# The first tile's load of a rotary-embedding kernel, issued as two partition halves on two DMA queues

## The chip, the core and the metric

The kernel runs on one core of one Trainium2 chip. The metric is the device time of one execution in microseconds (us). Repeated executions (five of the kernel before) took 162.28 to 162.43 us. Kernels are compared only within the same rounds. The span of the profiled execution is about 2 us shorter than the time (160.4 us against 162.38).

## The reference

Each of 16 x 512 positions holds 16 heads of 64 numbers (float32). The first 32 numbers of a head are rotated with a cosine and a sine of the position; the last 32 pass through.

```python
batch, seq, heads, dim = (16, 512, 16, 64)          # x: 33.5 MB
x1, x2 = x[..., :32], x[..., 32:]
rotated_first  = x1[..., :16] * cos[..., :16] - x1[..., 16:] * sin[..., :16]
rotated_second = x1[..., :16] * sin[..., :16] + x1[..., 16:] * cos[..., :16]
return concatenate([rotated_first, rotated_second, x2], axis=-1)
```

## The kernel before

x is cut into 8 tiles of 4 MiB. A tile in SBUF, the core's on-chip memory, takes 128 partitions, with one contiguous row of 32 KiB in each. A tile is loaded whole, the rotated part is overwritten in place by VectorE, and the tile is stored whole. Five tile buffers exist. Loads go through the queue of SyncE ("first queue", q1 in the profile), stores through the queue of ScalarE ("second queue", q10); cos and sin (64 KiB each, 64 partitions) go first on the second queue.

```python
nc.scalar.dma_start(out=stage[:, 0]..., in_=cosf)      # 64 partitions, 1 KiB each
nc.scalar.dma_start(out=stage[:, 1]..., in_=sinf)
# ... four small VectorE copies spread them to `table` on 128 partitions ...
for t in range(T):                                     # T = 8
    x_t = x_pool.tile([P, K, H, D], fp32)              # bufs=5, P=128
    nc.sync.dma_start(out=x_t..., in_=xf[t])
    for k0 in range(0, K, KC):                         # two rounds per tile
        # mul, mul, sub, add on VectorE, in place in x_t
        ...
    nc.scalar.dma_start(out=of[t], in_=x_t...)
```

## Time and profile before

| | before |
|---|---|
| time | 162.38 us |
| span of the profiled run | 160.4 us |
| moved | 67.25 MB, mean 419 GB/s |
| VectorE busy | 110.8 us |
| first multiplication starts | 18.3 us |
| last multiplication group ends | about 142 us |

The page's slices show the span in 40 equal parts: busy tenths of VectorE (DVE) and of the DMA engines, and GB/s.

```profile
DVE  0001599999999999999998799609995099940000
DMA  7999999999999999999999999999999999999993
GB/s 253 408 400 408 392 417 490 400 408 498 400 400 474 433 392 457 457 392 449 466 392 417 490 400 408 498 400 400 476 425 400 466 441 400 449 457 400 417 482 147
```

DMA is full from the second slice to the last but one, VectorE is not. DMA sets the time. The start of the span, in the timeline (start us, duration us, engine, line, operation; in brackets the idle time before it and what ended it):

```profile
12.19 0.59 DVE L48 COPY table<-stage 64x256 f32<-64x256 f32 x2 [12.19 <-DMA stage<-in_cos_dram]
17.67 0.59 DVE L48 COPY table<-stage 64x256 f32<-64x256 f32 x2 [4.90 <-DMA stage<-in_sin_dram]
18.29 2.29 DVE L65 TENSOR_TENSOR a_t<-x_t,table 128x2048 f32<-128x2048 f32 x1
```

VectorE's first wait is for the tables, sin last. The tile view of x_t gives the landing times of the loads after their issue; the shortest is tile 0's:

```profile
DMA to landing us min/median/max: 12.9/33.9/57.6
```

It was issued at 0.73 us, so tile 0 is there at 13.6 us, before the sin table.

The trace also has a record of every DMA packet: queue, start, duration, size. A row of 32 KiB is one packet; the median packet takes 1213 ns, which is 27.0 GB/s on one of the 16 DMA engines. A tile is 8 packets on each engine, so 16 transfers of a tile need 16 x 8 x 1.213 = 155.3 us of the span. The records carry no engine number. But between the first large packet and the last, 16 of them were under way at once for 145.6 of 157.5 us (17 to 19 for 5.6 us), so the engines can be followed as 16 chains of packets, one behind the other.

The chain of waits (start, duration, what) runs through VectorE, which is no contradiction: it follows releases, and all of these DMA pieces are spent in full queues.

```profile
1.30 16.34 DMA stage<-in_sin_dram
59.83 34.11 DMA out_dram<-x_t
93.99 34.21 DMA x_t<-in_x_dram
```

### The profile page before, as it was taken

Reading aid. Unit: us, or ns where it says so; the run is one execution under the profiler, and the core shown is the slowest. Engines: PE = TensorE matmul, PEld = TensorE weight load, DVE = VectorE, ACT = ScalarE, POOL = GpSimd, SP = SyncE. Lnnn points to the kernel's source line nnn. Section 1 sums busy time; section 2 is a strip of 40 time slices with the busy share of each in tenths; the row PEclk is TensorE's granted clock in tenths of the full one; section 3 lists DMA queues with packets and bytes.
Section 4 is the critical chain, followed back from the end, with each engine's and each line's share of the span. In section 5 each row is a group of like instructions: output and inputs, shape, how many; then the busy total and the mean of one; then the engine's idle time right before and its main releaser. Section 6 shows DMA issues by size and latency. Waiting matters only on the chain.

```text
span 160.4 us, 155 instructions
## 1 busy us (share of the span) xinstructions
DVE 110.8 (69%) x68; POOL 0.2 (0%) x4
## 2 busy tenths in 40 slices
DVE  0001599999999999999998799609995099940000
POOL 0000000000000000000000000000000000000000
DMA  7999999999999999999999999999999999999993
GB/s 253 408 400 408 392 417 490 400 408 498 400 400 474 433 392 457 457 392 449 466 392 417 490 400 408 498 400 400 476 425 400 466 441 400 449 457 400 417 482 147
DMA packets 2465, 67.25 MB, mean 419 GB/s; under 512 B 288, under 2 KB 416, under 8 KB 416
## 3 DMA queue, kind: packets, MB, share of 16 engines
q1 hardware_dynamic: 1152, 33.55, 49.3%
q10 hardware_dynamic: 1312, 33.69, 48.7%
q14 instruction: 1, 0.01, 0.0%
HBM read 33.69 MB, written 33.55 MB: 419 GB/s over the span
## 4 chain that ended last, share of the span: by engine, by line
DMA 53%; DVE 30%; issue 4%; DVEq 1%; ACTq 0%; SPq 0%
DMA x_t<-in_x_dram 21%; DMA out_dram<-x_t 21%; DVE b_t L66 11%; DMA stage<-in_sin_dram 10%; DVE a_t L65 10%; DVE x_t L70 5%; DVE x_t L67 4%; DVEq L99 1%; ACTq L41 0%; DVE table L48 0%; SPq L58 0%; DVEq L65 0%
## 5 line engine op out<-in xcount | busy, mean ns | idle before, releaser
L65 DVE TENSOR_TENSOR a_t<-x_t,table 128x2048 f32<-128x2048 f32 x16 | 36.7, 2292 | 13.6 <-DMA x_t<-in_x_dram 13.2
L66 DVE TENSOR_TENSOR b_t<-x_t,table 128x2048 f32<-128x2048 f32 x16 | 36.5, 2284 | 0.0
L67 DVE TENSOR_TENSOR x_t<-a_t,b_t 128x1024 f32<-128x1024 f32 x16 | 19.6, 1226 | 0.6
L70 DVE TENSOR_TENSOR x_t<-a_t,b_t 128x1024 f32<-128x1024 f32 x16 | 19.5, 1218 | 0.0
L48 DVE COPY table<-stage 64x256 f32<-64x256 f32 x4 | 1.1, 287 | 17.1 <-DMA stage<-in_cos_dram 12.2
L88 POOL MEMSET const-bfloat16-1.0<- 128x1 bf16 x1 | 0.1, 102 | 0.0
L88 POOL MEMSET const-uint8-127<- 128x1 uint8 x1 | 0.1, 102 | 0.0
L88 POOL MEMSET const-float32-0.0<- 128x1 f32 x1 | 0.1, 99 | 0.2 <-issue 0.2
L88 POOL MEMSET const-float32-1.0<- 128x1 f32 x1 | 0.1, 99 | 0.0
## 6 DMA issues: line engine op xcount, KB each, us to landing
x_t<-in_x_dram SPq DMA_DIRECT2D x8, 4096.0 KB, 33.9
out_dram<-x_t ACTq DMA_DIRECT2D x8, 4096.0 KB, 31.3
stage<-in_cos_dram ACTq DMA_DIRECT2D x1, 64.0 KB, 11.4
stage<-in_sin_dram ACTq DMA_DIRECT2D x1, 64.0 KB, 16.3
```

The lines of the kernel that those rows point to most:

```text
L48: nc.vector.tensor_copy(out=table[r * PB : (r + 1) * PB, t], in_=stage[:, t, :, 0:Q].unsqueeze(2).to_broadcast((PB, K, 2, Q)),)
L65: nc.vector.tensor_mul(out=a_t[:], in0=x1, in1=c)
L66: nc.vector.tensor_mul(out=b_t[:], in0=x1, in1=s)
L67: nc.vector.tensor_sub(out=x1[:, :, :, 0:Q], in0=a_t[:, :, :, 0:Q], in1=b_t[:, :, :, Q:HF])
L70: nc.vector.tensor_add(out=x1[:, :, :, Q:HF], in0=a_t[:, :, :, Q:HF], in1=b_t[:, :, :, 0:Q])
L88: nc = _bacc.Bacc("TRN2", target_bir_lowering=False, num_devices=1)
L99: with _tile.TileContext(nc) as tc:
```

## The change

Both queues are free at the start, and VectorE waits 18 us. The change hands half of tile 0 to each queue, so that it might arrive sooner; the tables now queue behind the second half.

```diff
+    x_0 = x_pool.tile([P, K, H, D], fp32, name="x_t")
+    for eng, lo in ((nc.sync, 0), (nc.scalar, P // 2)):
+        eng.dma_start(
+            out=x_0[lo : lo + P // 2].rearrange("p k h d -> p (k h d)"),
+            in_=xf[0, lo : lo + P // 2],
+        )
+
     stage = const_pool.tile([PB, 2, K, HF], fp32)
     nc.scalar.dma_start(out=stage[:, 0]..., in_=cosf)     # cut
     nc.scalar.dma_start(out=stage[:, 1]..., in_=sinf)
 ...
     for t in range(T):
-        x_t = x_pool.tile([P, K, H, D], fp32)
-        nc.sync.dma_start(out=x_t.rearrange("p k h d -> p (k h d)"), in_=xf[t])
+        if t == 0:
+            x_t = x_0
+        else:
+            x_t = x_pool.tile([P, K, H, D], fp32, name="x_t")
+            nc.sync.dma_start(out=x_t.rearrange("p k h d -> p (k h d)"), in_=xf[t])
```

## The prediction

> **What bounds the kernel now.** DMA throughput. The page's slices show DMA at 9 tenths or more in all but the first and last; 67.25 MB move at a mean of 419 GB/s. In the trace's packet records almost every 32768 B packet (one partition's row) takes 1213 ns, 27.0 GB/s per engine. There are 16 tile transfers of 8 such packets per engine: 16 x 8 x 1.213 = 155.3 us of the 160.4 us span; the rest is the start (first packet about 1.8 us in), the tables and the last landing. VectorE is busy 110.8 us, 13.9 us per tile against 19.4 us of DMA per tile. Its 18.3 us before the first multiplication and its later waits for x_t (13.2 us in the waits view) don't set the end.
>
> **What the change does.** The bytes stay. One load of 8 packets per engine becomes two of 4, plus 16 four-byte semaphore packets (9 ns each: nothing). One more issue costs 0.35 to 0.6 us on an idle sequencer.
>
> *Order.* Today cos lands at 12.2 us, sin at 17.6, x_0 at 13.6: the table, not x_0, ends the first wait. The queues' packets alternate one for one on an engine; sin took 5.5 us that way after cos. With half of x_0 ahead of them the tables come 4 large packets later. The change delays the very thing that VectorE waits for.
>
> *Rate.* A 64-partition load uses all 16 engines with 4 packets each (the trace shows this for the tables). [...] The engines start within about 0.6 us of each other, so they mostly stay in step. [...]
>
> **Critical path.** No later gap can absorb the loss, since DMA has none: all of it lands on the end. The late VectorE start costs nothing by itself: the tables should land near 33 us, VectorE start near 34, its last tile end near 145, and the last store's turn comes only at about 155. Five buffers (48.5 us of loads) keep DMA supplied until stores are queued.
>
> **Predicted: 169.5 us**, 8 in 10 between 163.0 and 172.0. Faster by over 2%: 0.01; within 2%: 0.19; slower by over 2%: 0.80.
>
> **What would show it.** Packets of the half loads at 2.0 to 2.5 us (right) or 1.2 us (wrong), later ones at 1.213; 220 to 260 GB/s in the slices from 4 to 18 us; x_0's landing near 22 us instead of 13.6; first multiplication near 34 us instead of 18.3; full DMA slices after that, VectorE's busy time unchanged, last store landing about 8 us later.
>
> **What would make it wrong.** [...] If VectorE starts far beyond 34 us, DMA runs dry near 70 us and it is worse.

(Passages are cut from the record: the ground for expecting that a load of one partition half is slow, which no trace had shown, and the loss taken from it. The cut term is what tile 0's eight half packets per engine lose. It came to 7 to 9 us by the author's estimate, at most 9.7, and 7.1 us of it entered the forecast: 162.38 + 7.1 = 169.5. The last paragraph named a smaller loss, 162 to 166 us, and none, for the case that this ground fails; that is cut too.)

## More of the kernel before

The DMA work of the first 26 us, by the windows view (stretch, its length, VectorE busy, GpSimd busy, clock, DMA share, GB/s; a packet counts whole in the stretch where it starts, so a share can exceed 1):

```profile
2.00:8.00 6.00, 0.00 (x0) 0.00 (x0) 1.00 0.91 382
8.00:14.00 6.00, 0.57 (x2) 0.00 (x0) 1.00 0.94 372
14.00:20.00 6.00, 2.28 (x3) 0.00 (x0) 1.00 1.04 431
20.00:26.00 6.00, 5.93 (x5) 0.00 (x0) 1.00 1.02 437
```

## The result

172.21 us against 162.38 us: 9.8 us, 6.1% slower (ratio 1.0607, 95% interval 1.0592 to 1.0621). A ratio here is the mean time of one kernel's fast runs over that of the other's of the same rounds, so not quite the ratio of the medians that are quoted. The profiled run's span is 170.5 us.

The same slices after the change:

```profile
DVE  0000000659999999999999999999997699500000
DMA  6999799989898999999999999999999898999993
GB/s 161 215 238 246 161 358 449 415 377 484 377 484 384 476 392 469 400 461 407 453 407 453 407 461 415 446 430 432 453 400 484 377 484 384 477 392 469 400 461 131
```

DMA is nearly as full as before, but in slices 2 to 5 (4.3 us each) it moves 161 to 246 GB/s in place of about 400. From slice 7 on it moves about what it did. A busy share alone would have hidden the loss; the GB/s line beside it shows it. The timeline of the start:

```profile
30.38 0.59 DVE L55 COPY table<-stage 64x256 f32<-64x256 f32 x2 [30.38 <-DMA stage<-in_cos_dram]
31.00 2.29 DVE L75 TENSOR_TENSOR a_t<-x_t,table 128x2048 f32<-128x2048 f32 x1
35.79 0.59 DVE L55 COPY table<-stage 64x256 f32<-64x256 f32 x2 [2.49 <-DMA stage<-in_sin_dram]
36.41 2.29 DVE L76 TENSOR_TENSOR b_t<-x_t,table 128x2048 f32<-128x2048 f32 x1
```

The tables come 18 us later than before, and VectorE starts 12.7 us later. The DMA issues (line omitted by the view; KB each, us from issue to landing) show the halves:

```profile
x_t<-in_x_dram SPq DMA_DIRECT2D x1, 2048.0 KB, 19.7
x_t<-in_x_dram ACTq DMA_DIRECT2D x1, 2048.0 KB, 23.2
stage<-in_cos_dram ACTq DMA_DIRECT2D x1, 64.0 KB, 29.0
stage<-in_sin_dram ACTq DMA_DIRECT2D x1, 64.0 KB, 33.6
```

Issued at 0.73 us, the halves land at 20.4 and 23.9 us; the whole tile used to land at 13.6. The windows:

```profile
2.00:8.00 6.00, 0.00 (x0) 0.00 (x0) 1.00 1.16 262
8.00:14.00 6.00, 0.00 (x0) 0.00 (x0) 1.00 0.92 202
14.00:20.00 6.00, 0.00 (x0) 0.00 (x0) 1.00 1.10 235
20.00:26.00 6.00, 0.00 (x0) 0.00 (x0) 1.00 0.92 350
```

And the packet records of tile 0's load (the first 8 large packets of each engine, 128 in all):

```
                        median packet   sum of the 8 per engine
before, whole tile          1215 ns         10.50 us
after, lower half           2384 ns          9.33 us  (4 packets)
after, upper half           2399 ns          9.71 us  (4 packets)
```

So the same 4 MiB took 19.04 us of every engine in place of 10.50: 8.5 us more. Over the whole trace, packets took 1.37 us per engine more than 1213 ns each before the change and 10.60 us more after it. That difference, 9.2 us, is nearly all of the 10.1 us by which the two spans differ. Of it, 8.5 us are the halves; the other 0.7 us lies in the loads behind them: tile 1's packets lost 0.4 us more per engine than before (its first on each engine, just behind the halves, took 1.5 to 2.4 us), tile 2's 0.2 us more.

The chain of waits again: it goes through the same kinds of DMA pieces, later, and the last of them is 9 us shorter.

```profile
2.21 33.55 DMA stage<-in_sin_dram
75.74 32.63 DMA out_dram<-x_t
108.44 24.98 DMA x_t<-in_x_dram
```

### The profile page after: what moved, and what is told of

It is laid out like the page before. It is cut to its first block, busy times and chain, and to the rows that moved or that the text cites. A ratio compares the mean times of both kernels' runs of the same rounds, so it can differ in the third digit from the quotient of the medians.

```text
span 170.5 us, 155 instructions
## 1 busy us (share of the span) xinstructions
DVE 110.9 (65%) x68; POOL 0.2 (0%) x4
## 4 chain that ended last, share of the span: by engine, by line
DMA 53%; DVE 27%; issue 4%; ACTq 1%; DVEq 1%; SPq 0%
DMA stage<-in_sin_dram 20%; DMA out_dram<-x_t 19%; DMA x_t<-in_x_dram 15%; DVE b_t L76 10%; DVE a_t L75 8%; DVE x_t L80 5%; DVE x_t L77 4%; DVEq L109 1%; ACTq L48 0%; DVE table L55 0%; ACTq L42 0%; SPq L68 0%; DVEq L75 0%
## 5 line engine op out<-in xcount | busy, mean ns | idle before, releaser
L55 DVE COPY table<-stage 64x256 f32<-64x256 f32 x4 | 1.1, 287 | 32.9 <-DMA stage<-in_cos_dram 30.4
L77 DVE TENSOR_TENSOR x_t<-a_t,b_t 128x1024 f32<-128x1024 f32 x16 | 19.6, 1226 | 0.6
```

What stands on the lines that cost most here:

```text
L55: nc.vector.tensor_copy(out=table[r * PB : (r + 1) * PB, t], in_=stage[:, t, :, 0:Q].unsqueeze(2).to_broadcast((PB, K, 2, Q)),)
L77: nc.vector.tensor_sub(out=x1[:, :, :, 0:Q], in0=a_t[:, :, :, 0:Q], in1=b_t[:, :, :, Q:HF])
```

## The experiments

Four explanations stood against each other. PORTS, here and in the labels of e13 and e14 a name only: which partitions a load writes sets its rate, so the packets of one partition half are slow (2384 and 2399 ns above) and, DMA having no gap, the whole loss reaches the end. The name and the ranges under it come from an assumption on why partitions matter; no run shows where on the chip the limit sits. ORDER: the tables, and so VectorE, being late costs the time. QUEUES: two load streams at once, or loads of 2 MiB, are slow. SHAPE: any load of fewer than 128 partitions is slow. All results were correct.

| run | what | time, us | before, same rounds | ratio |
|---|---|---|---|---|
| e1_tables_ahead | halves, tables ahead | 172.72 | 162.32 | 1.0635 |
| e2_whole_behind | whole tile on queue 2, tables behind | 164.28 | 162.32 | 1.0114 |
| e3_column_halves | halves by columns, two queues | 162.69 | 162.32 | 1.0021 |
| e4_one_queue | partition halves, one queue | 172.48 | 162.32 | 1.0623 |
| e5_offset32 | 32-95; 0-31; 96-127 | 168.12 | 162.40 | 1.0365 |
| e6_eighths | eight loads of 16 partitions | 189.16 | 162.40 | 1.1644 |
| e7_stagger | the change, 8 engines delayed | 173.81 | 162.40 | 1.0703 |
| e8_no_stagger | control of e7 | 173.46 | 162.40 | 1.0676 |
| e9_whole_tables_ahead | before, tables ahead of tile 0 | 164.00 | 162.37 | 1.0103 |
| e10_stagger2 | the change, 2 engines delayed | 172.93 | 162.37 | 1.0649 |
| e11_even_odd | halves by even and odd partitions | 162.80 | 162.37 | 1.0024 |
| e12_store_halves | before, tile 0's store in halves | 167.36 | 162.37 | 1.0307 |
| e13_one_port | before + loads of 2 neighbouring rows | 174.79 | 162.44 | 1.0760 |
| e14_two_ports | control of e13, rows four apart | 167.19 | 162.44 | 1.0296 |
| e15_stagger_two | e7 with two extra loads | 178.15 | 162.44 | 1.0991 |
| e16_halves_beside_whole | both halves on queue 2, tile 1 on queue 1 | 179.06 | 162.40 | 1.1037 |
| e17_mid_halves | before, tile 6's load in halves | 170.57 | 162.41 | 1.0509 |
| e18_mid_even_odd | before, tile 6's load even and odd | 162.45 | 162.41 | 1.0002 |

### Halves without late tables, and late tables without halves

```diff
 # e1_tables_ahead, against the change
+    nc.sync.dma_start(out=stage[:, 0]..., in_=cosf)      # ahead of the lower half
+    nc.sync.dma_start(out=stage[:, 1]..., in_=sinf)
     for eng, lo in ((nc.sync, 0), (nc.scalar, P // 2)): ...
-    nc.scalar.dma_start(out=stage[:, 0]..., in_=cosf)
-    nc.scalar.dma_start(out=stage[:, 1]..., in_=sinf)
```

> The change, with both table loads moved to the first queue ahead of the lower half, so that only the halves are left of it. Theory PORTS[...]: the half packets stay at about 2.4 us and the time stays at 171.5 to 172.5 us although VectorE starts earlier (the tables land by about 8 us, the first multiplication starts near 25 us instead of 31.0). Rival ORDER (the loss comes from the tables, and so VectorE, being late): the time falls by about as much as VectorE starts earlier, to 163 to 167 us.

```diff
 # e2_whole_behind, against the change
-    for eng, lo in ((nc.sync, 0), (nc.scalar, P // 2)):
-        eng.dma_start(out=x_0[lo : lo + P // 2]..., in_=xf[0, lo : lo + P // 2])
+    nc.scalar.dma_start(out=x_0[0:128]..., in_=xf[0, 0:128])
```

> Order alone: the first tile in one 128-partition load on the second queue, tables behind it, the later tiles on the first queue. PORTS: every 32768 B packet at 1.213 us, time 162.0 to 163.0 us, although the tables land late (cos near 28 us, sin near 33 us) and the first multiplication starts near 28 us instead of 18.3. ORDER: 170 to 173 us.

In e1 the first multiplication starts 6.6 us earlier than in the change, and the time is no better: 172.72 us. (The sin table still came only at 14.2 us, not by 8 as expected.) In e2 VectorE starts nearly as late as in the change, and the time is 164.28 us. From the two timelines, e1 first:

```profile
24.37 2.29 DVE L76 TENSOR_TENSOR a_t<-x_t,table 128x2048 f32<-128x2048 f32 x1 [9.61 <-DMA x_t<-in_x_dram]
```

```profile
28.95 0.59 DVE L55 COPY table<-stage 64x256 f32<-64x256 f32 x2 [28.95 <-DMA stage<-in_cos_dram]
29.57 2.29 DVE L75 TENSOR_TENSOR a_t<-x_t,table 128x2048 f32<-128x2048 f32 x1
```

Median half packets in e1 were 2559 and 2549 ns; tile 0's packets in e2 1213 ns. ORDER falls: a start at 29.6 us costs at most 2.0 us, and an earlier start gives nothing back.

The 2.0 us in e2 were not expected. The records place them: between 60 and 80 us after the first packet, packets took 1.8 us per engine longer than 1213 ns (before the change: none there). Those are 16 store packets and some 35 load packets at 1.3 to 2.4 us, around the point where loads resumed at 62.5 us (the issue in the timeline) after a pause in which only stores ran. Why resuming costs that was not tested.

### The same split in another direction, and on one queue

```diff
 # e3_column_halves, against the change
-        eng.dma_start(out=x_0[lo : lo + P // 2]..., in_=xf[0, lo : lo + P // 2])
+        eng.dma_start(out=x_0[:, k0 : k0 + K // 2]..., in_=xf[0, :, k0 * H * D : (k0 + K // 2) * H * D])
```

> Two halves of 2 MiB on the two queues, tables behind the second, as in the change, but each half has all 128 partitions and half the columns (16384 B per packet). PORTS: packets of 16384 B at about 0.61 us, time 162.0 to 163.5 us. Rival QUEUES (two load streams at once, or loads of 2 MiB, are slow in themselves): about 172 us, with packets at about 1.2 us. ORDER: between 165 and 172 us, since the tables still come behind a half.

```diff
 # e4_one_queue, against the change
-    for eng, lo in ((nc.sync, 0), (nc.scalar, P // 2)):
+    for eng, lo in ((nc.sync, 0), (nc.sync, P // 2)):
```

> Both partition halves on the first queue, one after the other; tables alone on the second, as before the change. PORTS: half packets still about 2.4 us, 8 per engine, time 171.5 to 172.5 us. QUEUES in the form that two streams disturb each other: 162.4 us with packets at 1.213 us. ORDER: the tables alternate with half packets on their own queue and land earlier than in the change, so a time clearly below 172 us.

Column halves: 16384-byte packets with a median of 611 ns (26.8 GB/s), 162.69 us. Partition halves on one queue: median 2543 ns, 172.48 us. QUEUES falls on both sides: two queues and two loads are harmless, and one queue doesn't help. In e4 the tables landed at 16.7 and 25.1 us, in the change at 30.4 and 35.8, at about the same time in total: ORDER falls once more.

### Which partitions, and how many

```diff
 # e5_offset32, against the change
-    for eng, lo in ((nc.sync, 0), (nc.scalar, P // 2)):
+    for eng, lo, n in ((nc.sync, 32, 64), (nc.scalar, 0, 32), (nc.scalar, 96, 32)):
 # e6_eighths, against the change (tables stay alone on the second queue)
+    for eng, lo, n in ((nc.sync, 0, 16), (nc.sync, 16, 16), ..., (nc.sync, 112, 16)):
```

> The change with other cuts: partitions 32 to 95 in one 64-partition load on the first queue; 0 to 31 and 96 to 127 in two 32-partition loads on the second, tables behind. [...] PORTS: 4 packets per engine (32 to 95) at about 1.21 us, 4 at about 2.4 us, so half the loss: 166.5 to 168.5 us. Rival SHAPE (any load of fewer than 128 partitions is slow in itself): all 8 at about 2.4 us, about 172.3 us.

> The first tile in eight loads of 16 partitions, all on the first queue, tables alone on the second. PORTS: [...]a packet takes about 4.85 us, each of 8 packets loses 3.64 us: 162.4 + 29.1 = 191.5 us (190 to 193). SHAPE (below 128 partitions half the rate): about 172.3 us. A cost per extra DMA, 9.8 us for one more as in the change: about 162.4 + 7 x 9.8 = 231 us.

Which partitions go together was assumed for both ranges, and had not been shown. In e5 the loss is 5.7 us, a little over half of the change's 9.8. Its packets are slow side by side (1.2 to 2.2 us for partitions 32 to 95, median 1585 ns; median 2375 ns for the others), but each engine's last packet of 32 to 95, when the others were done, took 1215 to 1220 ns. SHAPE falls here: a 64-partition load can run at full rate. In e6 the packets took 4604 ns, 3.8 times 1213, and the time was 189.16 us, 2.3 us below what was expected, most of it (8 x 0.25 = 2.0 us) because a packet took 4.60 us and not 4.85, four times 1.213. The windows of e6 show it as a rate:

```profile
10.00:16.00 6.00, 0.00 (x0) 0.00 (x0) 1.00 1.25 140
16.00:22.00 6.00, 0.00 (x0) 0.00 (x0) 1.00 1.18 133
```

From the median packet, 16 x 32768 B / 4.604 us = 114 GB/s; in the change 16 x 32768 B / 2.384 us = 220 GB/s. A whole tile at 1213 ns gets 432 GB/s. So half of the partitions got half of that rate, and 16 neighbouring ones about a quarter.

### Two rows, two engines, nothing else

```diff
 # e13_one_port, against before; e14_two_ports has slice(0, 8, 4), slice(1, 8, 4), ...
     nc.scalar.dma_start(out=stage[:, 1]..., in_=sinf)
+    first = [x_pool.tile([P, K, H, D], fp32, name="x_t") for _ in range(5)]
+    for sl in (slice(0, 2), slice(2, 4), slice(32, 34), slice(34, 36)):
+        nc.scalar.dma_start(out=first[4][sl]..., in_=xf[4, sl])
```

> The kernel before, plus four extra loads of two 32 KiB rows each on the second queue behind the tables, partitions 0 and 1, 2 and 3, 32 and 33, 34 and 35[...], loaded again later with tile 4, so the result stays right. Each uses 2 engines. COUPLED: while these packets run, the packets of the other 14 engines[...] are stretched well above 1.213 us too (up to about 2.4 us), for some 8 to 15 us; the time is above the control's by 2 us or more. PAIRS: only the two engines have slow packets, the other 14 stay at 1.213 us, and the time is within 5 us of the kernel before only because two engines carry four packets more each.

> Control: the same four extra loads of two rows, but partitions 0 and 4, 1 and 5, 2 and 6, 3 and 7[...]. Both theories: all packets at 1.213 us (but for the first ones), the two engines carry 4 packets more each; time 162.4 to 167.5 us.

This measures the disputed cost alone. Two rows use two engines. With neighbouring rows (e13) the eight extra packets took 1851 to 2228 ns, median 2019; with rows four apart (e14), 1213 to 1225 ns. From 18.2 to 35 us, while these ran, the other 14 engines' packets took at most 1308 ns (1226 in the control), far from the 2.4 us of COUPLED, the idea that a conflict anywhere slows all engines. It falls.

Two more things are in these records. First, the packet that each of the two engines ran just after a slow one was slow too (1.42 to 1.86 us): the two records together lose about 1.2 us, spread over both. A record's length is thus not the cost of its own rows alone. Second, e14 has only two engines with 4 packets more, and it is 4.8 us slower: 4 x 1.213 = 4.85. There the engines with most to do set the end. In e13 the cost over the control is 7.6 us, more than the slow packets of either engine add up to (4.5 and 5.1 us). The records show where the rest went: from 151 to 157 us after the first packet only the two late engines were still busy, with packets of the second queue, that is of the store before the last; then none for 3 us while VectorE worked on the last tile, which it had only begun at 147.2 us of the span (137.4 in the control), and only then came the last store. In the control only the two engines were busy for about 3 us, and there was no such pause. The time range given for PAIRS (within 5 us of before) was wrong for that reason.

### Engines out of step

The prediction took less than the full loss because the engines start at different times (within about 0.6 us). That this gives relief was the assumption, and so was which engines slow each other two by two (PAIRS, partners in the expectations); neither had been shown. Three runs tried to force more relief.

```diff
 # e7_stagger, against the change: 8 rows of tile 1 first, on 8 engines
+    x_1 = x_pool.tile([P, K, H, D], fp32, name="x_t")
+    nc.sync.dma_start(out=x_1[0:32:4]..., in_=xf[1, 0:32:4])
 # e8_no_stagger: the same for every engine
+    nc.sync.dma_start(out=x_1[:, 0]..., in_=xf[1, :, 0 : H * D])
 # e10_stagger2: x_1[0:8:4];  e15_stagger_two: x_1[0:32:4] and x_1[1:32:4]
```

> The change, with one more load in front: 8 rows of the second tile (partitions 0, 4, ... 28, so 8 engines[...]), loaded again later with the rest, so the result stays right. It adds 8 packets of work and puts 8 engines one packet behind the other 8. PORTS[...]:[...] most half packets at 1.2 to 1.6 us, two or three slow ones left, time 163.5 to 167 us, faster than the change although it loads more. SHAPE[...]: 172.3 to 173 us.

> Control for the staggered run: the extra load in front is 4 KiB of each of 128 partitions (twice the bytes, the same for every engine), so no engine falls behind. PORTS: the half packets stay at about 2.4 us and the extra 512 KiB add about 1.2 us: 172.8 to 174.3 us. If any extra load in front helped, whatever its shape: below 170 us.

> The staggered run again with an extra load of 2 rows (partitions 0 and 4) in place of 8, so that only 2 engines start a packet behind. The run with 8 gave no relief[...]. PAIRS INSIDE: the 2 delayed engines and their 2 partners have half packets between 1.2 and 1.9 us in the records, the other 12 stay at about 2.4 us; the time stays near 172.3 us, since the 12 set the landing. NO STAGGER HELPS[...]: all half packets at about 2.4 us, also 172.3 us.

> The staggered run with two extra loads of 8 rows, so that 8 engines are about two packets (2.4 us, one slow packet) behind the other 8. PAIRS[...]:[...] half packets mostly 1.2 to 1.6 us, time 165 to 168 us. If [...]a conflict anywhere slows all: half packets at about 2.4 us, 173 to 175 us.

None gave relief. Of the 128 half packets none took under 1.7 us in any of the four runs; the medians are 2369 (e7), 2378 (e8), 2405 (e10) and 2536 ns (e15). But the runs are weak: the second queue had served its half packets first, so when the halves began to alternate the delayed engines were only about 1 us behind in e7 (0.1 to 1.8) and 1.2 to 2.3 us in e10, less than one slow packet. In e10 the two late engines had no relief even so. In e15 the groups were on opposite halves for one packet alone, right behind the second extra load, and that was the slowest of all (2.8 to 3.4 us); the run came out above its range. Two later runs put something else between the half packets.

```diff
 # e12_store_halves, against before
-        nc.scalar.dma_start(out=of[t], in_=x_t...)
+        for lo, n in ((0, 64), (64, 64)) if t == 0 else ((0, 128),):
+            nc.scalar.dma_start(out=of[t, lo : lo + n], in_=x_t[lo : lo + n]...)
 # e17_mid_halves, against before; e18: slice(0, P, 2), slice(1, P, 2)
-        nc.sync.dma_start(out=x_t..., in_=xf[t])
+        for sl in (slice(0, 64), slice(64, P)) if t == 6 else (slice(0, P),):
+            nc.sync.dma_start(out=x_t[sl]..., in_=xf[t, sl])
```

> The kernel before, with only the first tile's store cut into two partition halves, both on the second queue. If reading SBUF is limited[...] as writing is: store packets of that tile at about 2.4 us while loads between them stay near 1.2 us, time up by 5 to 9.7 us (167 to 172.5 us). If only writes are limited: 162.4 us, packets at 1.213 us.

> The kernel before; only the load of tile 6, which alternates with store packets, is cut into partitions 0 to 63 and 64 to 127, both on the first queue. STEP MATTERS: the lower half's packets are slow (about 2 to 2.4 us) and spread the engines, the upper half's run near 1.213 us as the upper half of the cut store did, loss 3 to 6 us: 165.5 to 168.5 us. STEP DOES NOT MATTER in loads: all 8 packets per engine about 2.4 us, 171 to 173 us.

A store cut in halves is slow too, so the choice of partitions counts in reading SBUF as well: after its first packet per engine, nearly all of the lower half's packets took 1.8 to 2.4 us. But by the upper half the engines had drifted 2 us apart, and with whole-tile loads between the store packets most of those 64 took 1213 ns, a few 1.3 to 1.6. (The load packets just behind each half took up to 2.8 us, so part of the halves' cost may be booked on them.) Loss 5.0 us. The load cut in halves in the middle (e17) was the same test for writes. Its upper half's packets had a median of 1911 ns, the lower half's 2093, the stores between them about 1370. Most engines had stayed in step: 14 of 16 began the upper half within 0.85 us of each other, and their first packets took 1.7 to 2.1 us. The two engines ahead of them, at work while most others were on store packets, took 1213 ns each. So packets out of step with the others did run at the full rate there, but few; being out of step was not enough, since later, when the engines were up to 3.4 us apart, packets still took 1.4 to 2.1 us. Loss 8.2 us of the 9.7 that 8 packets at twice the time would cost. Its windows, and below them those of its control e18:

```profile
88.00:94.00 6.00, 4.63 (x3) 0.00 (x0) 1.00 1.13 355
94.00:100.00 6.00, 5.97 (x4) 0.00 (x0) 1.00 0.97 268
```

```profile
88.00:94.00 6.00, 4.92 (x3) 0.00 (x0) 1.00 1.00 431
94.00:100.00 6.00, 5.97 (x4) 0.00 (x0) 1.00 1.00 431
```

The run before, e16, was meant as that test and did not decide it:

```diff
 # e16_halves_beside_whole, against the change
-    for eng, lo in ((nc.sync, 0), (nc.scalar, P // 2)):
+    for eng, lo in ((nc.scalar, 0), (nc.scalar, P // 2)):
```

> Both partition halves of tile 0 on the second queue with the tables behind them, whole tiles from tile 1 on on the first queue, so that on each engine a packet of a half alternates with a packet of a whole tile[...]. STEP MATTERS: the first half packets are slow, engines fall out of step, later half packets run near 1.213 us, loss about half of the change's: 165 to 169 us. STEP DOES NOT MATTER: all half packets about 2.4 us, loss as in the change, 171.5 to 173 us.

179.06 us, outside both ranges. Half packets had medians of about 2.3 us (2297 and 2343 ns), and most of the whole-tile packets between them (tiles 1 and 2) were slow as well, at 1.5 to 2.2 us; why was not shown. The cos table was there only at 45.3 us, and here VectorE's late start did cost DMA time: by the timeline the first store was issued at 62.75 us, the load that waited for its buffer at 75.54 us, and the second store after 76 us. The window between:

```profile
74.00:76.00 2.00, 1.97 (x3) 0.00 (x0) 1.00 0.00 0
```

VectorE is busy, DMA moves nothing for two microseconds.

### A split without a loss

```diff
 # e11_even_odd, against the change
-    for eng, lo in ((nc.sync, 0), (nc.scalar, P // 2)):
-        eng.dma_start(out=x_0[lo : lo + P // 2]..., in_=xf[0, lo : lo + P // 2])
+    for eng, lo in ((nc.sync, 0), (nc.scalar, 1)):
+        eng.dma_start(out=x_0[lo:P:2]..., in_=xf[0, lo:P:2])
```

> The change with even partitions (0, 2, ... 126) in one load and odd ones in the other. [...] PORTS, counted at each moment: half packets again about 2.4 us, 171.5 to 173 us. PORTS, counted over the whole load[...]: packets at 1.213 us, 162 to 163 us.

> Control, and a second look at the even and odd cut: the load of tile 6 as even and odd partitions on the first queue. If this cut is free of conflicts as it was for tile 0: packets at 1.213 us, 162.2 to 163.3 us. If tile 0 was luck: 165 to 172 us.

Even and odd partitions as two loads of 64: median packet 1213 ns on both queues, 162.80 us for tile 0 (one of four runs took 167.6 us and counts as slow) and 162.45 us for tile 6, ratio 1.0002. Number of loads, bytes, rows per load and queues are those of the change; only the choice of partitions differs. The windows of e11, where the change moved 202 to 262 GB/s:

```profile
4.00:10.00 6.00, 0.00 (x0) 0.00 (x0) 1.00 0.99 426
10.00:16.00 6.00, 0.00 (x0) 0.00 (x0) 1.00 1.02 440
```

The range for "counted at each moment" rested on the assumption of which rows an engine gets and which slow each other; at 162.80 us and 1213 ns a packet these runs contradict it, and don't tell in what.

One rival has no run of its own. Partition p always holds row p of its tile, so every regrouping of partitions regrouped the rows in HBM, the memory that x lies in, as well; a limit there with the same grouping would look the same. Two things speak against it. In e5 rows 32 to 95 lie in HBM just as rows 0 to 63 do, 2 MiB in one stretch, and their undisturbed packets took 1215 to 1220 ns. And in e9 the cos table, 64 KiB in one stretch of HBM, took 0.36 us from the start of its first packet to the end of its last, 181 GB/s, where 16 neighbouring rows, 512 KiB of HBM in one stretch, got 114 in e6. Loading rows into other partitions than their own would settle it; that was not run.

### Does an earlier start help at all?

```diff
 # e9_whole_tables_ahead, against before
+    nc.sync.dma_start(out=stage[:, 0]..., in_=cosf)      # then tile 0 whole, same queue
+    nc.sync.dma_start(out=stage[:, 1]..., in_=sinf)
-    nc.scalar.dma_start(out=stage[:, 0]..., in_=cosf)
-    nc.scalar.dma_start(out=stage[:, 1]..., in_=sinf)
```

> What the change was after, without the halves: both tables ahead on the first queue, then the first tile in one 128-partition load, nothing but stores on the second queue. PORTS (the end is set by DMA packets alone): the first multiplication starts near 14 us instead of 18.3, every large packet at 1.213 us, and the time stays at 162.0 to 162.9 us. ORDER (an earlier VectorE start shortens the kernel): 158 to 160 us.

The start came as expected:

```profile
14.67 2.29 DVE L76 TENSOR_TENSOR a_t<-x_t,table 128x2048 f32<-128x2048 f32 x1 [10.51 <-DMA x_t<-in_x_dram]
```

It is 3.6 us earlier than before, and the time is 164.00 us, 1.6 us longer. By the records, engines were less busy in the first two microseconds, while the small table packets went first (0.7 us lost), the first packet started 0.3 us later, and packets were 0.4 us slower in sum; the rest was not traced. What the change was after is worth nothing here even when it is reached.

No run beat the kernel before.

## Why the prediction was wrong in size and right in kind

- "DMA throughput" bounds the kernel: right. The slices after are about as full as before, VectorE's busy time is 110.9 us against 110.8, and e1, e2 and e9 move VectorE's start between 14.7 and 29.6 us without the time following it.
- "The change delays the very thing that VectorE waits for": right, and without weight, as it said. The tables landed at 30.4 and 35.8 us (predicted near 33), the first multiplication started at 31.0 (predicted 34), the last VectorE work ended at 147.3 (predicted near 145).
- Packets of the half loads at 2.0 to 2.5 us, later ones at 1.213: right, 2384 and 2399 ns, but for the loads just behind the halves (tile 1's first packets: 1.5 to 2.4 us). GB/s from 4 to 18 us: predicted 220 to 260, measured 202 to 262 in the windows from 2 to 20 us. The halves landed at 20.4 and 23.9 us (predicted near 22). That the choice of partitions is the cause is what e3, e5, e11, e13 and e14 show: packets were slow in loads of one partition half (2384 and 2399 ns) and of two neighbouring rows (median 2019), and not for their bytes, queues or number of loads. Where on the chip the limit sits was not shown, and how engines slow each other from moment to moment stays open (e10, e11, e17).
- "All of it lands on the end": right. Packets account for 9.2 us of a difference of 10.1 us in the spans.
- **The step that failed** is the size: 7 to 9 us for tile 0's eight half packets per engine, taken as the whole loss. The prediction entered 7.1 us of it (169.5 against 162.38); 9.8 were measured. Two terms were mis-sized. First, the discount from the doubling of all eight (8 x 1.213 = 9.7 us): a median half packet lost 1.17 to 1.19 us, nearly the full factor of two. The sum, 19.04 us in place of 10.50, still came out at 8.5 us, inside "7 to 9", but only because tile 0's first packets were slow before the change too (0.8 us per engine), which the prediction did not count on. Second, nothing was allowed beside the eight packets ("later ones at 1.213"): tiles 1 and 2 lost another 0.7 us, the first packet started 0.3 us later, and gaps between an engine's packets grew by 0.5 us. Together 10.0 of the 10.1 us between the two spans.
- The discount came from reading start times in the records as the engines' step ("The engines start within about 0.6 us of each other"). In the change, the rounds of 16 half packets on one queue began within 0.8 to 1.7 us. In the change, the rounds of 16 half packets on one queue began within 0.8 to 1.7 us. No stagger run got a half packet under 1.7 us; in e17 the few packets well out of step ran at 1213 ns, and the load as a whole still lost 8.2 us. e13 shows why the reading was unsound: the packet behind a slow one was slow too (1.42 to 1.86 us), so a record doesn't show its own packet's cost alone. In e12's upper half the middle 12 engines were spread over 1.5 us, in e17's first upper packets 14 were within 0.85 us; whether that is why the one was relieved and the other hardly stays open.
- The range, 163.0 to 172.0 us, ended 0.2 us below the median. Its upper end left 9.6 us, about the doubling of all eight packets (9.7 us) with nothing else added. An upper end at that doubling was too tight.
- "If VectorE starts far beyond 34 us, DMA runs dry near 70 us": it did not in the change; e16, with the cos table at 45.3 us, shows it, at 74 to 76 us.

## What to carry to other kernels

When all DMA engines are busy, ask of a split not how early its first half arrives but whether every piece can still run at the full rate: a load of one half of the partitions (0 to 63 or 64 to 127) took twice the time per byte here (2384 and 2399 ns a packet in place of 1213), and most packets of a store's lower half nearly so (1.8 to 2.4 us), while column halves and even and odd partitions cost 0.3% or less (162.69 and 162.80 us against 162.32 and 162.37). In this kernel, bound by DMA, time lost in the first 20 us was not made up later, and an earlier start of the computing engine bought nothing. Read the GB/s line beside the busy line: here DMA counted as 7 to 9 tenths busy while it moved 161 to 246 GB/s.
